# A decoder trunk on one core: the down weights' upper and lower bits made by DMAs, and the LoRA factors' work paced differently

## The chip, the cores and the metric

The kernel runs on one core of one Trainium2 chip. The metric is the device time of one execution in microseconds (us). One execution of the kernel was also recorded by the hardware profiler; all rows of the profile below come from that execution.

## The reference

A trunk of two layers over 512 tokens of 1024 channels, in float32. Layer 0 mixes by a gated linear recurrence, layer 1 by RWKV-7; after each mixer comes a gated feed-forward network (FFN), and at the end a norm. The change touches the FFN and, by their pace, the LoRA factors of layer 1 (`w1`, `a1`, `g1` and their second factors).

```python
def _conv_ffn(x, norm, w_up, conv_w, conv_b, w_down):
    h = _rmsnorm(x, norm)
    u = jnp.einsum('btd,df->btf', h, w_up)
    gate = _causal_dwconv(u[..., :D_FF], conv_w, conv_b)
    hid = jax.nn.gelu(gate, approximate=True) * u[..., D_FF:]
    return jnp.einsum('btf,fd->btd', hid, w_down)
```

`w_up` is 1024 x 6144, `w_down` 3072 x 1024, in each layer.

## The kernel before

**Products in two parts.** TensorE multiplies fp32r, a type that keeps fewer bits than float32. Every operand is therefore kept as two fp32r tiles, upper bits (`wh`, `xh`) and lower bits (`wl`, `xl`), and `mm3` (L49) issues three matmuls into one accumulator, at L53 in the profile: wh·xh, wh·xl, wl·xh. `split` (L91) makes the two parts of a float32 tile: ScalarE (ACT) casts it into the upper tile (L93), VectorE (DVE) subtracts that from the source into the lower tile (L96).

**The weights' plan.** `plan_weights` (L99) lists all weight tiles of the program in the order in which they are used, 128 partitions x 1024 numbers (512 KB) each. Three counters run along the list. `weights_load` (L152) issues a DMA from SyncE's queue (SP) into a buffer `raw`; `weights_split` (L161) takes a raw tile and makes `wh` and `wl` of it; `next_weights` (L177) hands the next tile to a product, after having loaded to three ahead of it and split to two ahead. All of these buffers, and those of the halves below and of the LoRA factors, come from one ring of 21 buffers (`b4`, L83): a new tile takes a buffer that an earlier one held, and its first writer waits for that buffer's last readers.

**The FFN.** `ffn` (L556) walks over twelve pairs n of 256 hidden channels. Pairs 0, 1, 2, 4, 6, 8, 10 are done in whole products (accG and accU); pairs 3, 5, 7, 9, 11 (`HALVES`) by a scheme of seven products of half size, in the order 1, 5, 6, 2, 7 and then 4, 3, with accumulators accA, accF, accA, accD, accA and accA, accF. Their four quarter tiles of weights are loaded by the plan, but the parts `hi` and `lo` of each of the seven are made at L711 (ACT) and L712 (DVE).

After product 7 of each of the pairs 3, 5, 7, 9, 11 stands a stage of the product down, `down` (L784): it multiplies the hidden channels of the pairs before (four blocks of 128, after pair 11 eight) with their rows of `w_down` and adds to x. It has two halves of columns, g = 0 and 1; a tile holds two blocks of one half, so a stage takes four tiles, the last one eight. After the first tile of g = 0, products 4 and 3 of the pair come in between (`between`), then the rest. That makes ten stages and 48 down tiles over both layers. In layer 0 the stage is written by `project` and `project_gen` (L186, L214; weights stationary, matmuls at L53), in layer 1 out in `down` (hidden channels stationary, L805 to L807).

**Who sets the order.** Each engine works through its own instructions in program order and waits at semaphores; a scheduler puts the instructions of one engine in order by the readiness that it computes. At product 7 of a pair `weights_split(quads[n] + 6)` has the first two down tiles split.

**The LoRA factors.** Before the last down stage of layer 0 a task `lora_weights` (L850) is pushed. It loads the LoRA factors, scales them on DVE (`lt`, L860) and splits them (`g<-lt` at L93). `project` advances such tasks by `rate` steps for each pair of k blocks that it has issued (`background`), two by default; what is left is done when the mixer of layer 1 needs it.

Of the kernel before, what the change touches and what calls it, by code (L numbers as in the profile page):

```python
# [7 lines left out]
F32 = mybir.dt.float32  # L8
F32R = mybir.dt.float32r
AF = mybir.ActivationFunctionType  # L10
ALU = mybir.AluOpType
# [4 lines left out]
P = 128  # L16
D = 1024
T = 512
KB = D // P
DFF = 3072  # L20
# [23 lines left out]
class Kernel:  # L44
# [54 lines left out]
    def plan_weights(self):  # L99
        I = self.I  # L100
        plan = []
        self.quads = []

        def add(w, r0, c0, k=2, quad=False):
            plan.append((w[r0 : r0 + k * P, c0 : c0 + D // k].rearrange("(k p) c -> p k c", p=P), k, quad))

        def full(w, groups, rows=8):
            for g in groups:
                for k in range(0, rows, 2):
                    add(w, k * P, g * 512)  # L110

        def ffn(l):
            up, dn = I["ffn_w_up"][l], I["ffn_w_down"][l]

            def gu(six):


                for n in range(2 * six, 2 * six + 2):
                    self.quads.append(len(plan))
                    i = int(n in HALVES)  # L120
                    for half, r in ((i, 0), (1 - i, 0), (0, 512), (1, 512)):
                        add(up, r, half * DFF + n * 256, 4, bool(i))

            def dd(row, n):
                for g in range(2):
                    for k in range(0, n, 2):
                        add(dn, row + k * P, g * 512)

            gu(0)
            for six in range(1, 6):  # L130
                gu(six)
                if six < 5:
                    dd((six - 1) * 512, 4)
            dd(2048, 8)

        full(I["lru_w_in"][0], [2, 3, 0, 1])
        full(I["lru_w_out"][0], [0, 1])
        ffn(0)
        for i in (1, 0):
            full(I["rwkv_w_rkv"][0, i], [0, 1])  # L140
        for g in range(4):
            for k in range(0, 8, 4):
                add(I["rwkv_w_rkv"][0, 2], k * P, g * 256, 4)
        for h in range(2):
            for g in range(4):
                add(I["rwkv_w_out"][0], h * 512, g * 256, 4)
        ffn(1)
        self.plan = plan
        self.loaded, self.splitted = {}, {}
        self.n_load = self.n_split = self.n_used = 0  # L150

    def weights_load(self, upto):  # L152
        while self.n_load < min(upto, len(self.plan)):
            i = self.n_load
            src, k, _ = self.plan[i]
            raw = self.b4(F32, (k, D // k), f"raw{i}")
            self.nc.sync.dma_start(raw, src)
            self.loaded[i] = raw
            self.n_load += 1

    def weights_split(self, upto, pin=False):  # L161
        while self.n_split < min(upto, len(self.plan)):
            i = self.n_split
            if self.plan[i][2]:
                self.n_split += 1
                continue
            self.weights_load(i + 1)
            raw = self.loaded.pop(i)
            k = self.plan[i][1]
            hi = self.b4(F32R, (k, D // k), f"wh{i}")  # L170
            lo = self.b4(F32R, (k, D // k), f"wl{i}")
            for j in range(k) if i == 0 else [slice(0, k)]:
                self.split(raw[:, j], hi[:, j], lo[:, j], pin=pin)
            self.splitted[i] = (hi, lo)
            self.n_split += 1

    def next_weights(self, ahead=2):  # L177
        while self.plan[self.n_used][2]:
            self.n_used += 1
        i = self.n_used  # L180
        self.weights_load(i + 3)
        self.weights_split(i + ahead)
        self.n_used += 1
        return self.splitted.pop(i)

# [370 lines left out]
    def ffn(self, l, xs, finish, after=None):  # L556
        nc, tc = self.nc, self.tc
        last = l == 1
        with tc.tile_pool(name=f"ffn{l}", bufs=1) as pool:
# [192 lines left out]
            quads = self.quads[l * 12 : l * 12 + 12]  # L752
            pairs, hids = {}, []
            kind = lambda n: Halves if n in HALVES else Whole
# [3 lines left out]
            def ahead(j):  # L758
                while made[0] < min(j, len(seq)):
                    n, p = seq[made[0]]  # L760
                    if n not in pairs:
                        pairs[n] = kind(n)(n)
                    pairs[n].weights(p)
                    made[0] += 1

            def products(upto, more=2):

                while True:
                    n, p = seq[at[0]]
                    at[0] += 1  # L770
                    ahead(at[0] + more)
                    pairs[n].product(p)
                    if p == "G0" and n + 1 in HALVES:
                        self.weights_load(quads[n] + 8)
                    if n == 0 and p in ("G0", "U0"):
                        start(int(p == "U0"))
                    if n == 1 and p == "U0":
                        op.update(operands())
                    if p == 7:
                        self.weights_split(quads[n] + 6)  # L780
                    if (n, p) == upto:
                        return

            def down(n, b0, blocks, between, then):  # L784

                final = n == 11
                pieces = blocks // 2
                for g in range(2):
                    if last:
                        pss = [self.bank(f"acc{o}") for o in range(4)]  # L790
                        end = final and g == 1
                        for cs in [range(pieces)] if g else [(i,) for i in range(pieces)]:
                            ws = [self.next_weights() for _ in cs]
                            if final and cs[0] == 1:
                                self.weights_split(len(self.plan))
                            for b in range(4):
                                s = slice(b * P, (b + 1) * P)

                                for m in (slice(0, 256), slice(256, 512)) if end and b == 3 else (slice(0, 512),):
                                    ps = (self.bank("acc4") if m.start else pss[b])[:, m]  # L800
                                    for c, (wh, wl) in zip(cs, ws):
                                        for k in range(2):
                                            kk = c * 2 + k
                                            hh, hl = hids[b0 + kk]
                                            nc.tensor.matmul(ps, hh[:, s], wh[:, k, m], start=kk == 0, stop=False)  # L805
                                            nc.tensor.matmul(ps, hl[:, s], wh[:, k, m], start=False, stop=False)  # L806
                                            nc.tensor.matmul(ps, hh[:, s], wl[:, k, m], start=False, stop=kk == blocks - 1)  # L807
                                    if cs[-1] == pieces - 1:
                                        m = slice(g * 512 + m.start, g * 512 + m.stop)
                                        nc.vector.scalar_tensor_tensor(xtok[:, b, m], ps, self.rs[:, b : b + 1], xtok[:, b, m], ALU.mult, ALU.add)  # L810
                                        if final:
                                            finish(b, m, xtok[:, b, :], pool)
                            if not g and cs[0] == 0:
                                between()
                        if not g:
                            then()
                    else:
                        def ev(o, ps):
                            b = g * 4 + o
                            xb = self.x[:, b, :]  # L820
                            nc.vector.tensor_tensor(xb, xb, ps, ALU.add)
                            if final:
                                finish(b, room)

                        def hook(c):
                            if not g and c == 0:
                                between()
                            elif not g and c == pieces - 1:
                                then()

                        self.project(hids, ev, kb=blocks, join=2 if g else 1, after=hook, x0=b0)

            rooms = []

# [890 lines left out]
```

## Time and profile before

| | |
|---|---|
| time, three runs | 1308.49, 1309.42, 1313.31 us; median 1309.42 |
| the profiled execution | 1307.3 us, of which the span 1305.6 |
| TensorE (PE) busy | 1278.2 us, 98% of the span |
| VectorE (DVE) busy | 962.1 us, 74% |
| ScalarE (ACT) busy | 666.6 us, 51% |
| GpSimd (POOL) busy | 66.7 us, 5% |
| loads of down tiles (SP) | 48 of 512 KB, 3.8 us from issue to landing |

The span is the time from the first to the last instruction. Busy times are sums over an engine's instructions; engines work side by side, so they do not add up. A row of a group of instructions names the line, the engine, the operation, what is written and read, how often, the busy time, the mean of one in ns, and the idle time of the engine ahead of them with what ended it. Tile names stand without their numbers there: `wh`, `wl` are the parts of a weight tile, `raw` its source, `hid` the hidden channels, `acc` an accumulator.

### The profile page before, as it was taken

Reading aid. Unit: us, or ns where it says so; the run is one execution under the profiler, and the core shown is the slowest. Engines: PE = TensorE matmul, PEld = TensorE weight load, DVE = VectorE, ACT = ScalarE, POOL = GpSimd, SP = SyncE. Lnnn points to the kernel's source line nnn. Section 1 sums busy time; section 2 is a strip of 40 time slices with the busy share of each in tenths; the row PEclk is TensorE's granted clock in tenths of the full one; section 3 lists DMA queues with packets and bytes.
Section 4 is the critical chain, followed back from the end, with each engine's and each line's share of the span. In section 5 each row is a group of like instructions: output and inputs, shape, how many; then the busy total and the mean of one; then the engine's idle time right before and its main releaser. Section 6 shows DMA issues by size and latency. Waiting matters only on the chain.

```text
span 1305.6 us, 22294 instructions
## 1 busy us (share of the span) xinstructions
PE 1278.2 (98%) x9267; PEld 1074.2 (82%) x9267; DVE 962.1 (74%) x1448; ACT 666.6 (51%) x1064; POOL 66.7 (5%) x114
## 2 busy tenths in 40 slices
PE   9999999999999998999999999899999999999998
PEld 8878888888888886876678888778889898988886
DVE  5988778767767678578989976768777676766754
ACT  6897554433434344348854557755645243434442
POOL 4000000000000000010001121120000000000000
PEclk9999999999999998999999999999999999999999
DMA  6323340515050514322312121222324241415041
GB/s 198 116 65 98 97 139 24 162 33 172 23 177 30 165 53 115 111 66 75 98 33 90 51 61 33 94 83 81 97 65 130 65 141 53 160 34 177 27 136 65
DMA packets 96708, 120.39 MB, mean 92 GB/s; under 512 B 9498, under 2 KB 70628, under 8 KB 96480
## 3 DMA queue, kind: packets, MB, share of 16 engines
q1 hardware_dynamic: 95248, 117.20, 28.4%
q8 instruction: 72, 1.18, 0.4%
q10 hardware_dynamic: 576, 1.05, 0.2%
q0 software_dynamic: 784, 0.74, 0.2%
q14 instruction: 28, 0.23, 0.1%
HBM read 114.44 MB, written 4.52 MB: 91 GB/s over the span
## 4 chain that ended last, share of the span: by engine, by line
PE 84%; DVE 9%; ACT 5%; issue 2%; POOL 0%; POOLq 0%; DVEq 0%; ACTq 0%
PE acc L53 25%; PE accU L53 12%; PE accG L53 12%; PE accA L53 8%; PE accF L53 4%; PE acc L807 3%; PE acc L806 3%; PE acc L805 3%; PE accD L53 2%; PE lg L53 1%; DVE X L1248 1%; DVE wl L96 1%; PE lwa L53 1%; DVE DA L1246 1%; PE s L1366 1%
## 5 line engine op out<-in xcount | busy, mean ns | idle before, releaser
L93 ACT CAST wh<-raw 128x1024 fp32r<-128x1024 f32 (+1 forms) x161 | 166.0, 1043 | 199.4 <-PE acc L53 51.4
L96 DVE TENSOR_TENSOR wl<-raw,wh 128x1024 fp32r<-128x1024 f32 (+1 forms) x161 | 194.1, 1213 | 91.4 <-ACT wh L93 75.7
L53 PE MATMUL accG<-xs,wh 128*128 128x512 f32 x448 | 138.8, 391 | 0.0
L53 PE MATMUL accU<-xs,wh 128*128 128x512 f32 x448 | 138.7, 391 | 0.0
L53 PE MATMUL acc<-hid,wh 128*128 128x512 f32 x384 | 121.8, 399 | 6.5 <-ACT wh L93 6.5
L53 PEld LDWEIGHTS accG<-xs,wh 128*128 128x128 f32 x448 | 83.7, 188 | 17.3
L53 PEld LDWEIGHTS accU<-xs,wh 128*128 128x128 f32 x448 | 83.7, 188 | 17.1
L53 PEld LDWEIGHTS acc<-hid,wh 128*128 128x128 f32 x384 | 72.0, 190 | 23.7 <-ACT wh L93 6.9
L53 PE MATMUL accG<-xs,wl 128*128 128x512 f32 x224 | 87.3, 390 | 0.0
L53 PE MATMUL accU<-xs,wl 128*128 128x512 f32 x224 | 87.3, 390 | 0.0
L53 PE MATMUL accA<-xt,hi 128*128 128x256 f32 x480 | 83.4, 277 | 0.0
L53 PE MATMUL acc<-xs,wh 128*128 128x512 f32 x256 | 80.2, 394 | 0.0
L658 DVE SCALAR_TENSOR_TENSOR cv<-gpad,pv,cv 128x512 f32<-128x512 f32 x96 | 69.1, 747 | 12.5 <-ACT cv L656 12.1
L712 DVE TENSOR_TENSOR lo<-raw,hi 128x1024 fp32r<-128x1024 f32 x40 | 48.3, 1221 | 40.2 <-PE accU L53 40.2
L807 PE MATMUL acc<-wl,hid 128*128 128x512 f32 (+1 forms) x200 | 77.2, 386 | 0.0
L806 PE MATMUL acc<-wh,hid 128*128 128x512 f32 (+1 forms) x200 | 77.0, 385 | 0.0
L805 PE MATMUL acc<-wh,hid 128*128 128x512 f32 (+1 forms) x200 | 76.7, 383 | 0.0
L53 PE MATMUL acc<-hid,wl 128*128 128x512 f32 x192 | 76.2, 398 | 0.0
L53 PEld LDWEIGHTS accA<-xt,hi 128*128 128x128 f32 x480 | 73.1, 188 | 0.9
L711 ACT CAST hi<-raw 128x1024 fp32r<-128x1024 f32 x40 | 42.0, 1050 | 57.7 <-PE accG L53 49.6
L53 PE MATMUL accA<-xt,lo 128*128 128x256 f32 x240 | 66.3, 276 | 0.0
L53 PE MATMUL acc<-mix,wh 128*128 128x512 f32 x192 | 60.3, 399 | 0.0
(411 smaller groups left out, 3001.1 us busy)
## 6 DMA issues: line engine op xcount, KB each, us to landing
raw<-in_ffn_w_up_dram SPq DMA_DIRECT2D x96, 512.0 KB, 3.6
raw<-in_ffn_w_down_dram SPq DMA_DIRECT2D x48, 512.0 KB, 3.8
raw<-in_rwkv_w_rkv_dram SPq DMA_DIRECT2D x24, 512.0 KB, 3.9
raw<-in_lru_w_in_dram SPq DMA_DIRECT2D x16, 512.0 KB, 4.1
raw<-in_lru_w_out_dram SPq DMA_DIRECT2D x8, 512.0 KB, 3.8
raw<-in_rwkv_w_out_dram SPq DMA_DIRECT2D x8, 512.0 KB, 3.5
xd<-x SPq DMA_DIRECT2D x8, 256.0 KB, 2.0
AR<-xd SPq DMA_DIRECT2D x1, 2048.0 KB, 8.5
```

The source lines that it names most:

```text
L53: mm = lambda *a, **kw: self.nc.tensor.matmul(ps, *a, skip_group_check=more, **kw)
L93: put = (self.nc.vector.tensor_copy if dve else self.nc.scalar.copy)(hi, src)
L96: self.nc.vector.tensor_tensor(lo, src, hi.bitcast(F32), ALU.subtract)
L658: nc.vector.scalar_tensor_tensor(cv, pair.gp[:, e, j : j + T], cw(j), cv, ALU.mult, ALU.add)
L711: nc.scalar.copy(hi, f[p])
L712: tt(lo, f[p], hi.bitcast(F32), ALU.subtract)
L805: nc.tensor.matmul(ps, hh[:, s], wh[:, k, m], start=kk == 0, stop=False)
L806: nc.tensor.matmul(ps, hl[:, s], wh[:, k, m], start=False, stop=False)
L807: nc.tensor.matmul(ps, hh[:, s], wl[:, k, m], start=False, stop=kk == blocks - 1)
L1246: nc.vector.tensor_tensor(w, A[:, s + 1 :, s : s + 1].to_broadcast([P, n, j]), X[:, s : s + 1, 0:j].to_broadcast([P, n, j]), ALU.mult)
L1248: nc.vector.tensor_tensor(X[:, s + 1 :, 0:j], X[:, s + 1 :, 0:j], w, ALU.add)
L1366: nc.tensor.matmul(pss[h][half(z), b, col], w, AR[H][half(h), b, c2, q * P + col.start : q * P + col.stop], start=True, stop=True, tile_po ...
```

## The change

Entries of the plan get a kind. The quarter tiles of the halves are `"quad"` as before; the down tiles are `"dma"`, and both of their parts are made with the help of DMAs from GpSimd's queue. The upper part comes by a DMA from DRAM into an fp32r tile, which casts on its way. For the lower part ScalarE writes the upper part times -1 into a second tile, and a DMA from DRAM with `accum_op=add` adds the source onto it. Such a tile takes two buffers of the ring rather than three. The loads of down tiles leave SP's queue, and the 48 casts (L93) and 48 subtracts (L96) are gone; 48 multiplications on ACT and 96 DMAs on POOL's queue come in their place.

The pace changes with it: at product 6 of a pair in halves the four down tiles behind it are loaded, and at product 7 three of them are split rather than two; `next_weights` loads six ahead and splits four ahead where the entry four ahead is a down tile. In `project` the last down stage of layer 0 advances the background tasks by 0.5 steps rather than by 2.

```diff
-        def add(w, r0, c0, k=2, quad=False):
...
+        def add(w, r0, c0, k=2, kind=None):
...
                     for k in range(0, n, 2):
-                        add(dn, row + k * P, g * 512)
+                        add(dn, row + k * P, g * 512, 2, "dma")
...
-            raw = self.b4(F32, (k, D // k), f"raw{i}")
-            self.nc.sync.dma_start(raw, src)
+            raw = self.b4(F32R if kind == "dma" else F32, (k, D // k), f"raw{i}")
+            (self.nc.gpsimd if kind == "dma" else self.nc.sync).dma_start(raw, src)
...
+            if self.plan[i][2] == "dma":
+
+                src, k, _ = self.plan[i]
+                hi, lo = self.loaded.pop(i), self.b4(F32R, (k, D // k), f"wl{i}")
+                self.nc.scalar.mul(lo, hi.bitcast(F32), -1.0)
+                self.nc.gpsimd.dma_start(lo, src, accum_op=ALU.add)
+                self.splitted[i] = (hi, lo)
+                self.n_split += 1
+                continue
...
         i = self.n_used
-        self.weights_load(i + 3)
-        self.weights_split(i + ahead)
+
+        far = i + 4 < len(self.plan) and self.plan[i + 4][2] == "dma"
+        self.weights_load(i + (6 if far else 3))
+        self.weights_split(i + (4 if far else ahead))
...
+                    if p == 6:
+                        self.weights_load(quads[n] + 8)
                     if p == 7:
-                        self.weights_split(quads[n] + 6)
+                        self.weights_split(quads[n] + 7)
...
-                        self.project(hids, ev, kb=blocks, join=2 if g else 1, after=hook, x0=b0)
+                        self.project(hids, ev, kb=blocks, join=2 if g else 1, rate=0.5 if final else 2, after=hook, x0=b0)
```

The sequence of products on TensorE is the same. Inside the first tile of a down stage it differs. Layer 0, the stage after pair 7, whose four tiles are numbers 64 to 67; TensorE's rows before, from the end of product 7 (`accA`) on:

```order
L53 MATMUL accA_3076<-xt_1477,lo7_3133 128x256
L53 MATMUL acc0_3237<-hid_2520,wh64_3227 128x512 [waits Activation_49]
L53 MATMUL acc0_3237<-hid_2520,wh64_3227 128x512
L53 MATMUL acc0_3237<-hid_2520,wl64_3228 128x512 [waits DVE_49]
L53 MATMUL acc0_3237<-hid_2520,wh64_3227 128x512 x2
L53 MATMUL acc0_3237<-hid_2520,wl64_3228 128x512
L53 MATMUL acc1_3238<-hid_2520,wh64_3227 128x512 x2
```

The same place after the change; `raw64` is now the upper part itself, and DMASW stands for a semaphore of a DMA from GpSimd's queue:

```order
L53 MATMUL accA_3068<-xt_1477,lo7_3125 128x256
L53 MATMUL acc0_3234<-hid_2516,raw64_3154 128x512 [waits DMASW4_49]
L53 MATMUL acc0_3234<-hid_2516,raw64_3154 128x512
L53 MATMUL acc1_3235<-hid_2516,raw64_3154 128x512 x2
L53 MATMUL acc2_3236<-hid_2516,raw64_3154 128x512 x2
L53 MATMUL acc3_3237<-hid_2516,raw64_3154 128x512 x2
L53 MATMUL acc0_3234<-hid_2516,wl64_3225 128x512 [waits DMASW0_49]
```

Before, the third matmul reads lower bits, and the accumulators come one after the other. Now eight matmuls that read upper bits, two for each of the four accumulators, stand ahead of the first one that reads lower bits.

ScalarE's queue at that stage before, from the cast for product 3 on (`s` is the copy of product 7 out of its accumulator):

```order
L711 CAST hi3_3193<-S4_2983 128x1024 [waits DVE_49]
L730 COPY s_3160<-accA_3076 128x512 [waits PE_49]
L93 CAST wh64_3227<-raw64_3225 128x1024 [waits DMAHW2_49,DVE_49]
L93 CAST wh65_3233<-raw65_3231 128x1024 [waits DMAHW3_49]
L730 COPY s_3221<-accA_3076 128x512 [waits PE_49]
L93 CAST wh66_3338<-raw66_3241 128x1024 [waits DMAHW4_49]
```

And after (line 172 is the multiplication, line 722 is 711 before, line 741 is 730 before):

```order
L741 COPY s_3152<-accA_3068 128x512 [waits PE_49]
L722 CAST hi3_3193<-S4_2975 128x1024 [waits DMASW3_49]
L172 ACTIVATE wl64_3225<-raw64_3154 128x1024 [waits DMASW4_49,PE_49,Activation_49]
L172 ACTIVATE wl65_3228<-raw65_3156 128x1024 [waits DMASW5_49,PE_49]
L172 ACTIVATE wl66_3231<-raw66_3158 128x1024 [waits DMASW6_49,DVE_49]
L741 COPY s_3221<-accA_3068 128x512 [waits PE_49]
```

The casts became multiplications that wait for the casting DMA and, for the buffer they write, for TensorE (product 2's upper bits, which `accD` reads), and the copy of product 7 stands behind three of them. On GpSimd's queue, where there was nothing between two norms, the stage now reads:

```order
L157 DMA raw64_3154<-in_ffn_w_down_dram 128x2x512 [waits DMASW4_49,DVE_49,PE_49]
L157 DMA raw65_3156<-in_ffn_w_down_dram 128x2x512 [waits DMAHW3_49,DMAHW2_49,DMAHW6_49,DMASW5_49,PE_49]
L157 DMA raw66_3158<-in_ffn_w_down_dram 128x2x512 [waits DMASW6_49,DVE_49]
L157 DMA raw67_3160<-in_ffn_w_down_dram 128x2x512 [waits DMAHW0_49,DMAHW5_49,DMASW7_49,PE_49]
L173 DMA wl64_3225<-in_ffn_w_down_dram 128x2x512 [waits DMAHW4_49,DMASW0_49,Activation_49]
L173 DMA wl65_3228<-in_ffn_w_down_dram 128x2x512 [waits DMASW1_49,Activation_49]
L173 DMA wl66_3231<-in_ffn_w_down_dram 128x2x512 [waits DMASW2_49,Activation_49]
```

All four casting DMAs stand ahead of the first accumulating one (L173), which waits for ScalarE's multiplication of the same tile.

More of the change, by code (lines that the diff above doesn't have):

```diff
@@ L102, in plan_weights @@
         self.quads = []
-        def add(w, r0, c0, k=2, quad=False):
-            plan.append((w[r0 : r0 + k * P, c0 : c0 + D // k].rearrange("(k p) c -> p k c", p=P), k, quad))
+        def add(w, r0, c0, k=2, kind=None):
+            plan.append((w[r0 : r0 + k * P, c0 : c0 + D // k].rearrange("(k p) c -> p k c", p=P), k, kind))
         def full(w, groups, rows=8):
@@ L121, in gu @@
                     for half, r in ((i, 0), (1 - i, 0), (0, 512), (1, 512)):
-                        add(up, r, half * DFF + n * 256, 4, bool(i))
+                        add(up, r, half * DFF + n * 256, 4, "quad" if i else None)
             def dd(row, n):
@@ L154, in weights_load @@
             i = self.n_load
-            src, k, _ = self.plan[i]
-            raw = self.b4(F32, (k, D // k), f"raw{i}")
-            self.nc.sync.dma_start(raw, src)
+            src, k, kind = self.plan[i]
+            raw = self.b4(F32R if kind == "dma" else F32, (k, D // k), f"raw{i}")
+            (self.nc.gpsimd if kind == "dma" else self.nc.sync).dma_start(raw, src)
             self.loaded[i] = raw
@@ L163, in weights_split @@
             i = self.n_split
-            if self.plan[i][2]:
+            if self.plan[i][2] == "quad":
                 self.n_split += 1
@@ L177, in next_weights @@
     def next_weights(self, ahead=2):
-        while self.plan[self.n_used][2]:
+        while self.plan[self.n_used][2] == "quad":
             self.n_used += 1
         i = self.n_used
-        self.weights_load(i + 3)
-        self.weights_split(i + ahead)
+        far = i + 4 < len(self.plan) and self.plan[i + 4][2] == "dma"
+        self.weights_load(i + (6 if far else 3))
+        self.weights_split(i + (4 if far else ahead))
         self.n_used += 1
```

## The prediction

> **What bounds the kernel now.** I read the page's busy times first, then its chain of waits, then the windows of a few stages, and last the timeline of one place. The page's busy times:
>
> ```profile
> PE 1278.2 (98%) x9267; PEld 1074.2 (82%) x9267; DVE 962.1 (74%) x1448; ACT 666.6 (51%) x1064; POOL 66.7 (5%) x114
> PE 84%; DVE 9%; ACT 5%; issue 2%; POOL 0%; POOLq 0%; DVEq 0%; ACTq 0%
> ```
>
> TensorE (PE) is busy for 1278.2 of the span's 1305.6 us, and 84% of the chain that ended last is its. So relieving another engine is worth only what TensorE waits for it, and any new wait of TensorE counts in full. The windows (columns: microseconds, busy time and count of PE, weight loads, DVE, ACT, POOL, then clock, DMA share, GB/s) show an ordinary piece of the first FFN, pair 7 with its product down, and the piece around that FFN's last pair, 11:
>
> ```profile
> 330.00:394.00 64.00, 64.00 (x363) 55.78 (x362) 44.78 (x54) 25.11 (x31) 0.00 (x0) 1.00 0.31 100
> 502.00:520.00 18.00, 11.55 (x55) 9.01 (x54) 18.00 (x24) 10.33 (x13) 0.00 (x0) 0.83 0.38 121
> ```
>
> The ordinary stage has no gap at all: 64.00 us busy of 64.00, with DVE at 44.78. The other is the one place in the FFNs where TensorE waits long. Its timeline, TensorE's rows, then ACT's, then SP's queue:
>
> ```profile
> 510.02 0.40 PE L53 MATMUL acc<-hid,wl 128*128 128x512 f32 x1
> 516.86 2.07 PE L53 MATMUL acc<-hid,wh 128*128 128x512 f32 x4 [6.45 <-ACT wh L93]
> 518.91 0.80 PE L53 MATMUL acc<-hid,wl 128*128 128x512 f32 x1
> 519.51 1.05 PE L53 MATMUL acc<-hid,wh 128*128 128x512 f32 x2
> 520.36 0.83 PE L53 MATMUL acc<-hid,wl 128*128 128x512 f32 x2
> 521.03 0.63 PE L53 MATMUL acc<-hid,wh 128*128 128x512 f32 x2
> ...
> 514.82 1.04 ACT L93 CAST g<-lt 128x1024 fp32r<-128x1024 f32 x1 [1.76 <-DVE lt L860]
> 515.77 1.04 ACT L93 CAST wh<-raw 128x1024 fp32r<-128x1024 f32 x1
> ...
> 504.84 10.29 SPq L157 DMA_DIRECT2D raw<-in_ffn_w_down_dram  x4
> ```
>
> TensorE stands for 6.45 us until ACT has cast a down weight, and ACT did that late because it was casting LoRA factors that waited 1.76 us for DVE (L860). Behind the gap nine matmuls start in 4.17 us (516.86 to 521.03), where the chain further down has 24 in 5.59 us, 0.233 us each, 2.1 us for nine: they ran at half clock and lost 2.1 us more. The window's clock of 0.83 tells when that began: 17% of 18 us, 3.1 us, was lost, 1.6 us of it in the 3.1 us of work from 516.86 to 520, so 1.5 us in the gap, which is its last 3.0 us at half clock. The clock fell 3.4 us into the gap.
>
> **The change part by part.** *What it takes away.* 48 subtracts and 48 casts of down weights, priced by these groups (mean ns of one behind the comma):
>
> ```profile
> L93 ACT CAST wh<-raw 128x1024 fp32r<-128x1024 f32 (+1 forms) x161 | 166.0, 1043 | 199.4 <-PE acc L53 51.4
> L96 DVE TENSOR_TENSOR wl<-raw,wh 128x1024 fp32r<-128x1024 f32 (+1 forms) x161 | 194.1, 1213 | 91.4 <-ACT wh L93 75.7
> ```
>
> DVE loses 48 × 1.213 = 58 us; ACT loses 48 × 1.043 = 50 us and gets 48 multiplications by -1. Both lie beneath the gapless matmuls of the first window, so I cost them at nothing; TensorE covers them already, and giving DVE more room moves no matmul.
>
> *The LoRA stall.* With the rate of 0.5 the factors come later on ACT and DVE, and the fourth down tile's upper bits no longer need ACT at all. The 6.45 us gap should go, with the half clock: -6.45 - 2.1 = -8.5 us. What is late next there is the accumulating DMA, below.
>
> *The upper bits by a casting DMA.* They leave SP for POOL's queue, are asked for during product 1, and the first is read after product 7. The chain of waits in the ordinary stage (start, us, what; products 1, 5, 6, 2, 7, then the down's first tile, then products 4 and 3, then the rest):
>
> ```profile
> 352.29 2.87 PE accA L53 x24
> 355.17 2.74 PE accF L53 x24
> 357.90 2.72 PE accA L53 x24
> 360.62 2.86 PE accD L53 x24
> 363.49 2.74 PE accA L53 x24
> 366.22 5.59 PE acc L53 x24
> 371.82 2.73 PE accA L53 x24
> 374.54 2.86 PE accF L53 x24
> ```
>
> The load's buffer is free when product 1's upper bits have been read, by about 355; the multiplication needs it at 363.49 (below), TensorE at 366.22. So a casting load has 8.5 to 11 us. I cost it at nothing up to that; beyond, it adds to the stall.
>
> *The lower bits.* This decides. A tile's lower bits now take three steps in a row: ACT writes the negative of the upper bits into a buffer, a DMA on POOL's queue adds the source onto it, and only its landing frees TensorE. The buffer of the first tile of a stage is that of product 2's upper bits, so ACT cannot start before 363.49. From there: the multiplication, handing over, the DMA from issue to landing (call it L), less what TensorE has to do meanwhile: product 7, and the matmuls of the upper bits that now stand ahead of the first of the lower bits, eight of them. Eight cost 8 × 5.59 / 24 = 1.86 us. ACT's scaling into this type is shown only at half the size, beside a cast of that size:
>
> ```profile
> L296 ACT ACTIVATE xs<-x,pv 128x512 fp32r<-128x512 f32 x16 | 11.6, 724 | 28.3 <-DVE x L548 16.4 <-DVE x L1639 10.3 <-DVE gpad L566 1.6
> L93 ACT CAST hid<-s 128x512 fp32r<-128x512 f32 x28 | 17.4, 622 | 13.8 <-DVE s L688 7.6 <-DVE s L690 6.1
> ```
>
> 724/622 × 1.043 = 1.2 us; 0.1 us for the semaphores is my estimate. So the stall in a stage is 1.2 + 0.1 + L - 2.74 - 1.86 = L - 3.3 us.
>
> No accumulating DMA is in the trace. L is bounded by plain transfers of 512 KB: the down loads of SP's queue below, and the only large one of POOL's.
>
> ```profile
> raw<-in_ffn_w_down_dram SPq DMA_DIRECT2D x48, 512.0 KB, 3.8
> fg<-in_final_norm_dram POOLq DMA_DIRECT2D x1, 512.0 KB, 7.6
> L1668 POOL DMA_DIRECT2D fg<-in_final_norm_dram x1: 647/647/647, 1241.2 to 1241.2; - x1
> ```
>
> From below, L = 3.8 as on SP. From above, the fg row, 7.6, and more. Why POOL's is longer is seen in the queues' packets (window 1241.1 to 1244.2, then 1244.2 to 1248.8; packets, MB, share of the engines), and for SP's load issued at 357.98 in 358.9 to 361.7:
>
> ```profile
> q1 hardware_dynamic: 324, 0.62, 59.3%
> ...
> q1 hardware_dynamic: 408, 0.79, 51.7%
> q0 software_dynamic: 144, 0.52, 28.6%
> ...
> q1 hardware_dynamic: 275, 0.53, 63.6%
> ```
>
> The software queue moved nothing in the 3.0 us after the issue, and then shared the engines with two SP loads; SP's own load had no packet for about 1 us and landed 2.65 us after. Without company POOL's 512 KB would land in about 3.0 + 2.65 = 5.65 us. The accumulation also reads and writes its destination, for which no row has a price; in the first stage, four casting and three accumulating transfers share this queue. I take 7.6, the only row of this size and queue, its company standing for the second read: a stall of 4.3 us. Ten stages (n = 3, 5, 7, 9 and 11 in both layers) make 43 us. The later tiles of a stage start their multiplications right behind the first and have products 4 and 3, 5.59 us, as cover: nothing, unless the queue moves under one tile in 3 us.
>
> The Trainium skill prices it otherwise: the page "DMA: Bandwidth & Descriptors", section "Anatomy of one DMA — SWDGE (gpsimd) path", fits 2.0 us plus bytes over 436 GB/s to a DMA of this path, which for 512 KB is an estimate of 3.2 us. By that every stall of this part would be zero; the 3.0 us to the first packet above speak against it.
>
> *What stands behind the new waits.* On ACT the copy of product 7 (L730) comes after up to three multiplications: if all start at 363.49 it ends by 363.49 + 3.6 + 0.6 = 367.7, ahead of product 4 at 371.82; nothing. On POOL, behind the accumulations, stand only the norms' small steps (L323, L1684) and fg's load, needed in the final norm; nothing. SP has 48 loads fewer; the products' loads can only come earlier, and TensorE doesn't wait for them now.
>
> *The clock.* The gap above lowered it from 3.4 us on. A stall of 4.3 us passes that by 0.9 us; the gap of 6.45 us passed it by 3.0 us and lost 2.1 us. In proportion, an estimate, 0.6 us a stage: +6 us.
>
> *Sum.* The profiled execution took 1307.3 us (span 1305.6). 1307.3 + 43 + 6 - 8.5 = 1347.8. The median of before's three timed runs, 1309.4, is 2.1 us above the profiled one, so 1350 us.
>
> **The rivals.** *Faster: the DMA fits into its window* (L up to 3.3). No stall is left and only the LoRA gap's end remains: 1309.4 - 8.5 = 1301. For it: SP's queue takes 3.8 us, and the page's fit. Against it: the fg row and its first packet. It decides on the time from POOL's issue to the first packet: at 1 us as on SP there would be next to no stall. 0.09.
>
> *About no change:* L between 3.5 and 4.8, where ten stalls of 0.2 to 1.5 us and the 8.5 us about cancel: 1303 to 1316. For: POOL's first packet may come sooner when it has nothing else behind it. Against: it needs an accumulation hardly slower than SP's plain load. 0.08.
>
> *Much slower: the transfers themselves are long.* If casting or accumulating runs at half the pace or less, L is 10 and above, the four accumulations of a stage queue behind each other, and tiles two to four wait as well. With L = 10 a stall is 6.7 us and loses 2.3 us by the clock: 10 × 9.0 - 8.5 = +82, 1391 us; with queueing past 1400. For it: each byte is touched three times. Against it: nothing measured either way. 0.18.
>
> *The change does not do what it says:* the LoRA gap stays, because DVE's slices of L860 come due anyway. It would add 8.5 us to my forecast, 1358 us; it is inside the first case's range. *DVE relieved gives time:* speaks for it 91 us that DVE waits for ACT in the L96 row; against it the first window, where TensorE never waits for either. I give it no chance of its own.
>
> **How the numbers follow.** The forecast's own case, L from 4.8 to 10, has 0.65: 1316 to 1391, and likeliest at 7.6, 1350. Faster has 0.09, no change 0.08, much slower 0.18. A run of this kernel can tell about 0.5%, 6.5 us, from no change. The range leaves out the faster case and the upper half of the slowest: 1303 to 1405. Faster by over 0.5%: 0.09; within: 0.08; slower: 0.65 + 0.18 = 0.83.
>
> **What would show it.** In the profile after, TensorE's waits should name the accumulating DMA's landing (tile wl) ten times, each of L - 3.3 us, and the DMA list a landing of about 7.6 us for wl. The gap at 510 should name no ACT cast. DVE should lose 58 us. The sum is wrong if wl lands in under 4 us, if the first wait of a stage is on the upper bits, or if tiles two to four wait as long as the first.

## The result and the profile after

The changed kernel takes 1346.55 us (median of four runs, 1345.38 to 1347.33), the kernel before 1308.96 us (1308.49 to 1313.31): the ratio is 1.028, with a 95% interval of 1.0259 to 1.0302, 37.6 us more. The forecast was 1350, in a range from 1303 to 1405.

The page after has the same two lines of busy times and chain as were read before the change:

```profile
PE 1292.0 (96%) x9267; PEld 1082.4 (81%) x9267; DVE 906.9 (67%) x1400; ACT 664.2 (49%) x1064; POOL 160.7 (12%) x210
PE 57%; issue 25%; DVE 8%; ACT 5%; DMA 4%; POOL 1%; POOLq 0%; DVEq 0%; ACTq 0%
```

DVE lost 55 us and ACT stayed as it was, and neither shows in the time. A DMA now stands in the chain, with 4% of a span of 1343.7 us. The 25% called issue are time for which the profile names no cause, so I read nothing from PE's smaller share. The list of TensorE's waits names that DMA; its columns are the total in us, the number of waits and the longest:

```profile
PE acc L53 <- DMA wl<-in_ffn_w_down_dram: 16.6, 5, 4.2
PE acc L820 <- DMA wl<-in_ffn_w_down_dram: 14.5, 5, 3.4
PE pd L1461 <- ACT tu L1455: 4.6, 5, 2.1
...
PE acc L53 <- ACT wh L93: 0.2, 1, 0.2
```

Ten waits, one for each down stage, five in each layer, 31.1 us together; the old wait for ACT's cast, 6.7 us in this list before, is down to 0.2. The stage after pair 7 shows one of them in full. First ACT's timeline, then POOL's, then TensorE's:

```profile
373.89 2.96 ACT L172 ACTIVATE wl<-raw 128x1024 fp32r<-128x1024 f32 x3 [1.26 <-issue]
...
375.25 4.91 POOL L173 DMA_DIRECT2D wl<-in_ffn_w_down_dram  x4 [6.01 <-ACT wl L172]
...
376.50 2.02 PE L53 MATMUL acc<-hid,raw 128*128 128x512 f32 x8
381.32 0.79 PE L53 MATMUL acc<-hid,wl 128*128 128x512 f32 x1 [2.79 <-DMA wl<-in_ffn_w_down_dram]
381.91 1.05 PE L53 MATMUL acc<-hid,raw 128*128 128x512 f32 x2
```

The multiplication starts at 373.89, the accumulation is issued at 375.25, TensorE does product 7 and the eight matmuls of the upper bits and then stands until the tile has landed, 6.07 us after the issue. Over all ten stages the time from that issue to the first matmul of lower bits is 6.0 to 7.9 us, 6.5 on the mean. What comes behind the stall is seen in the windows of this stage (clock in the third column from the right):

```profile
374.00:378.00 4.00, 4.00 (x31) 3.73 (x30) 2.00 (x3) 4.00 (x5) 2.75 (x3) 1.00 0.18 18
378.00:381.00 3.00, 0.52 (x3) 0.09 (x1) 0.72 (x2) 0.28 (x1) 2.17 (x2) 1.00 1.05 212
381.00:384.00 3.00, 2.68 (x6) 2.15 (x7) 0.00 (x0) 0.00 (x0) 0.00 (x0) 0.52 1.05 237
384.00:386.00 2.00, 2.00 (x9) 1.59 (x8) 0.00 (x0) 0.00 (x0) 0.00 (x0) 0.86 1.13 208
```

A gap of 2.79 us was enough to halve the clock. It fell 2.62 us after the last matmul, at 381.14, and work was back 0.18 us later: 0.52 over three microseconds and 0.86 over two, 1.7 us lost.

The sum closes. TensorE's idle time went from 1305.6 - 1278.2 = 27.4 to 1343.7 - 1292.0 = 51.7 us, 24.3 more; 31.1 us of new waits less 6.5 of the old one are 24.6. Its busy time, for the same 9267 matmuls, went up by 13.8 us: slower matmuls behind the stalls, less those that used to follow the old gap. 24.3 + 13.8 = 38.1 us, the difference of the spans. The issue list gives the price of the transfers:

```profile
raw<-in_ffn_w_down_dram POOLq DMA_DIRECT2D x48, 512.0 KB, 6.1
wl<-in_ffn_w_down_dram POOLq DMA_DIRECT2D x48, 512.0 KB, 9.5
```

The 9.5 us are the median of all 48; the first of a stage lands in 6 to 8, those behind it queue.

### The profile page after: what moved, and what is told of

Its sections match the earlier page's. It is cut to its first block, busy times and chain, and to the rows that moved or that the text cites. A ratio compares the mean times of both kernels' runs of the same rounds, so it can differ in the third digit from the quotient of the medians.

```text
span 1343.7 us, 22436 instructions
## 1 busy us (share of the span) xinstructions
PE 1292.0 (96%) x9267; PEld 1082.4 (81%) x9267; DVE 906.9 (67%) x1400; ACT 664.2 (49%) x1064; POOL 160.7 (12%) x210
## 3 DMA queue, kind: packets, MB, share of 16 engines
q0 software_dynamic: 26896, 51.07, 17.5%
## 4 chain that ended last, share of the span: by engine, by line
PE 57%; issue 25%; DVE 8%; ACT 5%; DMA 4%; POOL 1%; POOLq 0%; DVEq 0%; ACTq 0%
PE acc L53 21%; PE accG L53 7%; PE accU L53 7%; DMA wl<-in_ffn_w_down_dram 4%; PE accA L53 2%; PE acc L820 2%; PE acc L819 2%; PE acc L818 2%; PE accF L53 2%; PE lg L53 1%; DVE X L1261 1%; DVE wl L96 1%; POOL raw L157 1%; PE lwa L53 1%; PE s L1379 1%
## 5 line engine op out<-in xcount | busy, mean ns | idle before, releaser
L96 DVE TENSOR_TENSOR wl<-raw,wh 128x1024 fp32r<-128x1024 f32 (+1 forms) x113 | 135.8, 1211 | 145.6 <-PE accA L53 86.8
L93 ACT CAST wh<-raw 128x1024 fp32r<-128x1024 f32 (+1 forms) x113 | 116.1, 1040 | 217.9 <-PE acc L53 61.4
L53 PE MATMUL acc<-hid,raw 128*128 128x512 f32 x384 | 123.3, 408 | 0.0
L157 POOL DMA_DIRECT2D raw<-in_ffn_w_down_dram x48 | 38.3, 837 | 573.6 <-PE accA L53 514.1
L53 PEld LDWEIGHTS acc<-hid,raw 128*128 128x128 f32 x384 | 74.9, 197 | 17.4
L819 PE MATMUL acc<-raw,hid 128*128 128x512 f32 (+1 forms) x200 | 78.3, 391 | 0.0
L818 PE MATMUL acc<-raw,hid 128*128 128x512 f32 (+1 forms) x200 | 78.1, 391 | 0.0
L173 POOL DMA_DIRECT2D wl<-in_ffn_w_down_dram x48 | 59.2, 1484 | 90.0 <-ACT wl L172 78.6
```

The lines of the kernel that those rows point to most:

```text
L53: mm = lambda *a, **kw: self.nc.tensor.matmul(ps, *a, skip_group_check=more, **kw)
L93: put = (self.nc.vector.tensor_copy if dve else self.nc.scalar.copy)(hi, src)
L96: self.nc.vector.tensor_tensor(lo, src, hi.bitcast(F32), ALU.subtract)
L157: (self.nc.gpsimd if kind == "dma" else self.nc.sync).dma_start(raw, src)
L173: self.nc.gpsimd.dma_start(lo, src, accum_op=ALU.add)
```

## The experiments

Eight kernels, each timed in the same session as the kernel before: 1 to 4 in one, where before took 1309.05 us, and 5 to 8 in another, on another chip, where it took 1308.69. The theory on trial, A, is that of the prediction: a stall is the start of the multiplication plus a landing of 6 to 7 us, and the old stall ended by the slower pace of the LoRA factors. The rival is named with each.

**1. The pace alone.** The kernel before, with one argument changed.

```diff
-self.project(hids, ev, kb=blocks, join=2 if g else 1, after=hook, x0=b0)
+self.project(hids, ev, kb=blocks, join=2 if g else 1, rate=0.5 if final else 2, after=hook, x0=b0)
```

> The kernel before with only the slower pace of the LoRA factors (0.5 in the last down stage of layer 0). Theory A (the pace alone ends the stall of 6.45 us and its half clock): 1309.0 - 8.5 = 1300.5 us, no wait of TensorE for the cast wh over 1 us. Theory B (the stall ends because the upper bits of the fourth tile no longer pass through ACT): the gap stays between 4 and 6.5 us, 1306 to 1309 us.

Measured: 1301.82 us (1300.35 to 1304.29), a ratio of 0.995 (0.9938 to 0.9962) to the kernel before. The windows of the two places where the old gap and its half clock lay:

```profile
502.00:520.00 18.00, 18.00 (x92) 14.91 (x92) 15.96 (x22) 8.31 (x11) 0.00 (x0) 1.00 0.22 60
...
520.00:552.00 32.00, 32.00 (x143) 25.82 (x142) 23.67 (x30) 15.77 (x23) 0.00 (x0) 1.00 0.51 160
```

18.00 us busy of 18.00 at full clock, where it had been 11.55 at 0.83. The pace is worth 7.2 us by itself, and this kernel is the fastest of the study.

**2. The DMAs at the old pace.** The changed kernel without its `rate`.

> The changed kernel with the LoRA factors at the old pace of 2. Theory A (the pace ended the old stall): a wait of about 6 us comes back in the last stage of layer 0, 1346.5 + 8 = 1354 us. Theory B (the casting load ended it): no such wait, 1346 to 1348 us.

Measured: 1356.24 us (1354.2 to 1356.74), 9.7 us over the changed kernel. The pace it is, in both directions. But the wait that came back has another name. TensorE's waits:

```profile
PE acc L53 <- DMA wl<-in_ffn_w_down_dram: 21.7, 7, 4.1
PE acc L820 <- DMA wl<-in_ffn_w_down_dram: 13.3, 5, 3.1
```

ACT's timeline in the last stage of layer 0:

```profile
542.73 1.05 ACT L93 CAST g<-lt 128x1024 fp32r<-128x1024 f32 x1 [1.44 <-DVE lt L873]
543.69 1.05 ACT L172 ACTIVATE wl<-raw 128x1024 fp32r<-128x1024 f32 x1
```

There are seven waits for `wl` in layer 0 rather than five, and the two new ones, of 1.65 and 4.10 us, are the 6 us that A forecast, in two pieces. In the first, a down tile's multiplication stands behind a LoRA cast on ACT just as its cast did before the change. The second is the next tile's, whose accumulation was issued at 548.84, with a casting load and the accumulation of the first tile still on the way, and landed 10.9 us later. Taking the upper bits off ACT did not end that stall; the lower bits' first step is still there.

**3. The first multiplication asked for at product 6.** Nothing else is changed; its buffer is then one that product 5 has read.

```diff
                     if p == 6:
                         self.weights_load(quads[n] + 8)
+                        self.weights_split(quads[n] + 5)
```

> The changed kernel with the first tile's multiplication and accumulation asked for at product 6 rather than 7; its buffer then comes free with product 5, so that it starts when the casting load has landed, some 2.2 us earlier. Theory A (the stall is the accumulation's start plus its 6 to 7 us): each of the ten stalls falls from 3.1 to about 0.9 us, and its half clock with it, 1346.5 - 22 - 10 = about 1314 us. Theory B (the transfers contend, and the landing is set by the bytes on the way): the landing moves by less than 0.7 us, 1338 us or more.

Measured: 1323.04 us (1319.29 to 1329.05). After pair 9 of layer 0 the accumulation is issued at 427.67, and TensorE's wait, here beside POOL's row, is small and without a half clock behind it (0.50 us is a matmul at full speed, 0.79 one at half):

```profile
427.67 1.21 POOL L173 DMA_DIRECT2D wl<-in_ffn_w_down_dram  x1 [2.16 <-ACT wl L172]
...
433.96 0.50 PE L53 MATMUL acc<-hid,wl 128*128 128x512 f32 x1 [0.58 <-DMA wl<-in_ffn_w_down_dram]
...
1064.74 0.50 PE L821 MATMUL acc<-wl,hid 128*128 128x512 f32 x1 [2.00 <-DMA wl<-in_ffn_w_down_dram]
```

The landing still takes 6.3 us; only its start moved, and the stall with it: 31.1 us of waits became 7.9. Theory A holds in kind: it had ten waits of 0.9 us, and they came to 7.9, though unevenly (two stages of layer 1 kept 2.0 and 1.6 us). It was 9 us too low in the sum. New waits for ACT's cast of hidden channels (1.8 and 2.3 us) came up in the last stages, and behind each the clock was half for 3.41 us (from 523.76 and from 1284.93); that makes 7.5 of the 9.

**4. Loads and first multiplication asked for at product 5.**

```diff
-                    if p == 6:
+                    if p == 5:
                         self.weights_load(quads[n] + 8)
+                        self.weights_split(quads[n] + 5)
```

> The changed kernel with the four casting loads asked for at product 5 and the first tile's multiplication at product 5 too, so that its accumulation can be issued some 4.9 us earlier. Theory A (start plus 6 to 7 us): it lands before TensorE reaches it, no stall of a first tile is left, and the half clock goes too; 1346.5 - 31 - 14 = about 1301 us, what the slower LoRA pace alone gives. Theory B (contention): stalls of 2 us and more stay, 1325 us or more.

Measured: 1309.8 us (twelve runs, 1302.36 to 1313.59), no change against before: ratio 0.9999 (0.9982 to 1.0017). The stalls on first tiles are gone: three waits of 0.35 to 0.56 us are left of ten, and the stage after pair 9 is gapless.

```profile
418.00:482.00 64.00, 64.00 (x365) 55.82 (x364) 40.44 (x52) 25.03 (x31) 7.70 (x8) 1.00 0.52 132
```

Of the 7.0 us by which its span is above that of experiment 1 (1308.6 against 1301.6), 4.3 come between the last stage's first matmul and TensorE's last, where its chain of waits makes a new detour (start, us, what):

```profile
1263.53 6.73 DMA raw<-in_ffn_w_down_dram
...
1270.37 1.06 ACT wl L172
1271.42 0.52 ACT hid L760
...
1271.96 0.70 DVE hid L761
...
1272.71 0.75 PE acc L821
```

A casting load was issued late on POOL's queue, 0.73 us behind an accumulation that had waited for ACT; a multiplication on ACT waited for the load, and the cast of the hidden channels, which needs neither and whose source was there from 1268.02 on, started when that multiplication ended. TensorE waited 2.05 us for it, and the clock was half for 3.41 us behind that (from 1272.78). Whether the load's buffer was free any sooner, no row tells. Why the runs of this kernel spread over 11 us I did not find out. The granted clock goes with the spread: it was 0.998 in the runs of 1302.36, 1304.86 and 1307.79 us and 0.992 to 0.995 in the five above 1310, and half a per cent of the time is 6.5 us. What moved the clock from run to run was not tried.

**5. A copy in place of the addition.** The second DMA writes the source instead of adding it. This kernel leaves the subtraction out, and its second tile holds the source rather than the lower bits; only its timing is read.

```diff
-                self.nc.gpsimd.dma_start(lo, src, accum_op=ALU.add)
+                self.nc.gpsimd.dma_start(lo, src)
```

> The changed kernel with the second DMA of a down tile copying the source onto the tile instead of adding it, on the same queue and after the same multiplication; the lower bits are left out of the result, the source stands in their place. Theory A (the landing is the software queue's own: it writes its descriptors before the first packet, whatever the operation): landing of a stage's first tile 5.5 to 6.5 us as now, stalls 2.5 to 3.1 us, 1338 to 1347 us. Theory B (reading and adding onto the destination is what is slow): landing about 4 us, stalls near 1 us, 1320 us or less.

Measured: 1313.1 us (1312.53 to 1317.36). Here theory A was wrong and its rival right. The ten waits shrink to 9.0 us, and no half clock follows. TensorE's waits:

```profile
PE acc L53 <- DMA wl<-in_ffn_w_down_dram: 4.7, 5, 1.0
...
PE acc L820 <- DMA wl<-in_ffn_w_down_dram: 4.3, 5, 1.0
```

What the trace has on the DMA's own line (busy time on POOL min/median/max in ns, then landings):

```profile
L173 POOL DMA_DIRECT2D wl<-in_ffn_w_down_dram x48: 703/713/721, 237.5 to 1270.7; - x48
...
DMA to landing us min/median/max: 3.9/6.1/9.0
```

And the same two lines of the changed kernel, which adds:

```profile
L173 POOL DMA_DIRECT2D wl<-in_ffn_w_down_dram x48: 1188/1512/2052, 237.9 to 1308.1; - x48
...
DMA to landing us min/median/max: 5.9/9.5/14.0
```

After pair 7 the copying DMA is issued at 367.06 and the first matmul of lower bits starts at 371.38, 4.3 us later, where the adding one took 6.07. A plain copy on this queue accounts for 4.3 us, the addition for about 2. Where these 2 us sit is in two rows: POOL's time for one issue doubles at the median, 0.71 to 1.51 us (for the first tile of a stage it is 1.2 us, half a microsecond more than the copy's); and the time of the software queue's packets, as a share of 16 engines' span and for the same packets and bytes, goes from this kernel's

```profile
q0 software_dynamic: 26896, 51.07, 13.4%
```

to the changed kernel's

```profile
q0 software_dynamic: 26896, 51.07, 17.5%
```

17.5% of 1343.7 us less 13.4% of 1310.8 us is 59.5 us, 1.24 us for each of 48 tiles.

**6. Upper bits alone by DMA.** The source comes by SP as well, and DVE subtracts.

```diff
-                hi, lo = self.loaded.pop(i), self.b4(F32R, (k, D // k), f"wl{i}")
-                self.nc.scalar.mul(lo, hi.bitcast(F32), -1.0)
-                self.nc.gpsimd.dma_start(lo, src, accum_op=ALU.add)
+                (raw, hi), lo = self.loaded.pop(i), self.b4(F32R, (k, D // k), f"wl{i}")
+                self.nc.vector.tensor_tensor(lo, raw, hi.bitcast(F32), ALU.subtract)
```

> The changed kernel with only the upper bits by a casting DMA; the source also comes by SP, and DVE subtracts as before the change. Theory A (the casting load is hidden and costs nothing, the stall is the accumulation's alone): no stall at a first tile, about 1302 us, what the slower LoRA pace alone gives. Theory B (a load on the software queue is late by itself): waits for the casting load or for DVE behind it in most stages, 1315 us or more.

Measured: 1305.48 us (1304.13 to 1310.1), ratio 0.9976 (0.9964 to 0.9989) to before. TensorE's list of waits has no entry for a down tile at all. The casting load is hidden although its median landing is later than the 3.8 us of the down loads before:

```profile
wh<-in_ffn_w_down_dram POOLq DMA_DIRECT2D x48, 512.0 KB, 6.9
```

That the kernel is still 3.7 us above experiment 1, which was timed in the other session, is named by no row; the profiled spans differ by 0.9 us only (1302.5 and 1301.6).

**7. Products 4 and 3 ahead of the first tile.** In `down`, `between()` is called before the first tile instead of behind it.

```diff
+                between()
                 for g in range(2):
...
-                            if not g and cs[0] == 0:
-                                between()
...
-                            if not g and c == 0:
-                                between()
-                            elif not g and c == pieces - 1:
+                            if not g and c == pieces - 1:
```

> The changed kernel with products 4 and 3 of the pair ahead of the first down tile instead of behind it, which gives the accumulation 5.6 us more cover. Theory A: no stall on wl is left; in its place product 4 waits for ACT's copy of product 7, which stands behind three multiplications, 0.5 to 1.5 us a stage and no half clock, 1346.5 - 31 - 16 + 10 = about 1309 us. Theory B (contention of the transfers): the landing moves out too and stalls of over 1.5 us stay, 1325 us or more.

Measured: 1304.83 us (1302.11 to 1309.6), ratio 0.9974 (0.996 to 0.9988) to before. Nine of ten stalls are gone, though the landings are as long as ever; the wait for ACT's copy of product 7 that A expected did not come up. TensorE's one wait for a down tile, and then the row of the issue list:

```profile
PE acc L821 <- DMA wl<-in_ffn_w_down_dram: 2.0, 1, 2.0
```

```profile
wl<-in_ffn_w_down_dram POOLq DMA_DIRECT2D x48, 512.0 KB, 9.9
```

So the whole chain of multiplication and accumulation can be hidden by 5.6 us of other products. What is then left is the gain of the pace, and nothing on top of it: DVE has 54 us less to do than in experiment 1 (906.9 against 961.0), and the time is 3 us longer rather than shorter (the two were timed in different sessions; their ratios to before are 0.9974 and 0.995).

**8. The gap filled with throwaway matmuls.** 15 matmuls, 3.5 us, ahead of the first tile of each stage, into the accumulator that the next matmul starts afresh.

```diff
+            self.filling = 15
...
+    def fill(self, ps, x):
+        for j in range(self.filling):
+            self.nc.tensor.matmul(ps, x[:, 0:P], x, start=True, stop=True)
+        self.filling = 0
```

> The changed kernel with 15 throwaway matmuls (3.5 us) ahead of the first tile of each stage, into the accumulator that the next matmul starts afresh; the scheduler then puts only two matmuls of upper bits ahead of the first of the lower bits, so six more are left for after the landing (1.4 us). Theory A (the gap itself brings the half clock, 1.6 us a stage): gaps below 1.5 us, no half clock in the stages, 1346.5 - 16 + 14 = about 1345 us in spite of 150 matmuls more. Theory B (the slow matmuls behind a stall come from the transfers beside them): they stay slow, 1346.5 + 14 = 1360 us.

Measured: 1353.37 us (1349.5 to 1354.97), between the two. The stage after pair 7 settles the question: no half clock behind the stall, against 0.52 and 0.86 in the changed kernel.

```profile
378.00:380.00 2.00, 2.00 (x10) 1.42 (x8) 0.34 (x1) 0.00 (x0) 1.72 (x2) 1.00 1.11 193
380.00:382.00 2.00, 1.16 (x6) 0.86 (x5) 0.00 (x0) 0.00 (x0) 0.00 (x0) 1.00 1.11 297
382.00:386.00 4.00, 4.00 (x19) 3.23 (x18) 0.00 (x0) 0.00 (x0) 0.00 (x0) 1.00 1.10 198
```

The DMA share is as high here (1.10 to 1.11) as beside the slow matmuls of the changed kernel, so it isn't the transfers that slow them. From the first wait of the stage after pair 5 to that after pair 7 this kernel needs 68.24 us and the changed one 68.18, though 15 matmuls more are done: A's sum, stage by stage. What A missed lies in the last stage: by pair 9 of layer 1 the two profiles are 1.3 us apart (1222.18 against 1220.87), at the end 6.9. There TensorE waited 2.11 us for the cast of hidden channels on ACT, the detour of experiment 4, and the one half clock of this kernel's down stages followed (from 1315.54).

## Why the prediction came out right

**The place and the mechanism held.** Ten stalls, one a stage, all for the accumulation's landing, on the first tile alone; the casting loads hidden (experiment 6); the later tiles hidden; nothing from 55 us less on DVE (experiment 7). That a stall is the multiplication's start plus a landing is shown by moving the start. In the stage after pair 7 the multiplication started 2.8 us before product 7 ended, in experiment 3 6.6 and in experiment 4 8.4 us before; only two matmuls of upper bits stand ahead of the first of lower bits there, not eight, which takes back 1.4 us. The waits went from 31.1 to 7.9 and 1.3 us, though the first tiles took no less time from issue to landing (6.7 and 7.1 us on the mean, 6.5 in the changed kernel).

**The landing was sized 1.1 us too long, and partly for a wrong reason.** I took 7.6 us from the fg row; the ten stages had 6.5. The formula, landing less 3.3 us, gives 3.2 us a stage with that, and 3.1 were measured: 31 us rather than 43. Its small terms held: multiplication and handing over took 1.36 us where it had 1.3. In the fg row the software queue moved nothing for 3.0 us, and I read that as the queue's own delay. The first packet came sooner here: in the stage after pair 7 at 377.18, 1.9 us after the issue, and in experiment 5 1.4 us after it, where the plain copy landed in 4.3 us. The rest, some 2 us, is the addition, which I had counted only as what might balance the company that fg had on the engines. The Trainium skill, page "DMA: Bandwidth & Descriptors", section "Anatomy of one DMA — SWDGE (gpsimd) path", makes the copy an estimate of 3.2 us; that is nearer to the 4.3 of experiment 5 than my 5.65, and 3.3 us short of the adding DMA's 6.5. With a plain copy the stalls would have been 0.9 us each and the kernel near no change.

**The clock was sized too small.** I let a gap of 4.3 us lose 0.6 us, since the old gap's clock had fallen only after 3.4 us. Stalls of 2.3 to 4.2 us lost about 1.6 us each on the mean: TensorE's busy time rose by 13.8 us, and the 2.1 us that went with the old gap come on top, 15.9 us for ten. Experiment 8 shows that the gap is the cause. The term that was mis-sized is the proportion. Windows of 20 us around three of the stalls of the changed kernel, those of 2.82, 3.99 and 3.02 us:

```profile
442.00:462.00 20.00, 17.18 (x105) 15.16 (x104) 4.70 (x7) 5.55 (x7) 4.89 (x4) 0.91 0.87 189
510.00:530.00 20.00, 16.01 (x91) 13.90 (x90) 5.15 (x8) 4.28 (x6) 7.18 (x7) 0.83 0.99 193
1010.00:1030.00 20.00, 16.98 (x109) 15.07 (x108) 3.76 (x5) 5.84 (x7) 4.90 (x4) 1.00 0.90 202
```

The loss is some 1.8, 3.4 and 0 us by these rounded clocks: lumps, not a share of the excess. The first kind followed seven stalls of the ten, the double one followed one, and two (3.02 and 2.26 us) had none.

The trace shows where the lumps come from. All changes of its clock lie on one raster of 3.41 us: the half clocks of the first five stalls begin at 244.61, 312.87, 381.14, 449.41 and 517.67, each 20 steps of 3.413 us after the one before. In the down stages a half clock lasts one step, or two, which loses up to 1.7 or 3.4 us. Here are two steps around the stall of 2.79 us, then two around that of 3.02 us:

```profile
377.73:381.14 3.41, 0.79 (x4) 0.31 (x2) 0.99 (x2) 0.55 (x1) 2.44 (x2) 1.00 1.00 205
381.14:384.55 3.41, 3.23 (x8) 2.56 (x9) 0.00 (x0) 0.00 (x0) 0.00 (x0) 0.50 1.07 228
...
1012.61:1016.02 3.41, 1.79 (x8) 1.13 (x6) 1.38 (x2) 1.56 (x3) 3.41 (x3) 1.00 0.83 130
1016.02:1019.43 3.41, 2.02 (x9) 1.68 (x10) 0.00 (x0) 0.00 (x0) 0.03 (x1) 1.00 0.97 235
```

The first stall left TensorE idle for 2.62 us of one step, and the next step ran at half clock. The other was cut by an edge into 1.62 and 1.39 us, and nothing followed. In the down stages of all these kernels, the steps that brought a half clock were idle for 1.89 us or more (the least in experiment 3, 1281.52 to 1284.93), and those that brought none for 1.68 us or less (experiment 3, 1063.07 to 1066.48). So, as an estimate from these two figures, a gap under 1.7 us is free of it, one over 3.8 us is not, and between them it depends on where the gap falls. Why the stall of 3.99 us cost two steps stays open.

**The two errors nearly cancel.** 12 us too much for the stalls and 10 too little for the clock; that 1350 came closer than its terms is luck.

**The old stall** went, as forecast, and by the pace alone (experiment 1, -7.2 us against -8.5). The other half of that step, that the upper bits' DMA frees the fourth tile from ACT, did nothing: in experiment 2 the wait came back through the lower bits' multiplication.

**The rivals.** The faster case needed a landing of 3.3 us; no form of this DMA got there. The much slower one needed the transfers at half pace; the addition makes a tile's packets 1.24 us longer, by the change of queue shares, and the tiles behind the first had room for it.

## What to carry to other kernels

A step that is moved from a busy engine to a DMA trades throughput for latency: where TensorE has no gap, the throughput was worth nothing, and the latency of the first tile of each stage is paid in full unless that tile's chain can start early. Ask when the chain's first step may start (here, which product frees its buffer), add the landing, and compare with the work that is there to cover it. When a change has two parts, time the small one alone: here all that could be gained lay in the one argument that paces the background work.

## What the runs showed of the hardware

An accumulating DMA of 512 KB from GpSimd's queue took 1.51 us to issue at the median where the copying one took 0.71, its packets took 1.24 us longer (their time summed over 16 engines and divided by 16), and the first of a stage landed about 2 us later, with the same packets and bytes. The clock halved after eight gaps of TensorE in the changed kernel's down stages, the shortest of 2.76 us, and did not after one of 3.02 us: length alone doesn't decide. It changed on a raster of 3.41 us, and a step of it idle for 1.89 us or more was followed by one at half clock, where 1.7 us were lost. The Trainium skill, page "TensorE: Matmul & The Clock Gate", section "Part 1: The HAM clock gate", says that the clock falls after at least one idle window of some 3.4 us, and that these windows run on by themselves, whenever work begins. The raster, and that the same gap may or may not cost, agree with the second half; the first is not borne out here, where gaps of 2.76 to 2.94 us were enough five times.
